# Scan of an RWKV-7 layer: 32x32 inverses from two 16x16 substitutions and two TensorE products, chunk products on 64 rows

## The chip, the cores and the metric

The kernel runs on one core of a Trainium2 chip. The metric is the time of one execution in microseconds (us) on the device. PE is the matrix engine, PEld its weight loads, DVE, ACT and POOL the vector, scalar and GpSimd engines, SP the engine whose queue issues most of the DMAs. Each engine takes its instructions in the order in which they stand for it, and waits on semaphores for the others.

## The reference

One inference step of a two-layer trunk: layer 0 mixes tokens with a bidirectional RWKV-7 scan, layer 1 with neighbourhood attention, each is followed by an MLP. There are 128 prompt tokens and 512 sample tokens, 16 heads of 64. What the change touches is the scan, run forward and backward:

```python
def delta_rule_scan(r, w, k, v, kk, a, s0, reverse):
    def step(S, inp):
        sa = jnp.einsum('bhvk,bhk->bhv', S, -kk_t)
        S_new = (S * w_t[:, :, None, :] + sa[..., None] * (kk_t * a_t)[:, :, None, :]
                 + v_t[..., None] * k_t[:, :, None, :]).astype(S.dtype)
        y = jnp.einsum('bhvk,bhk->bhv', S_new, r_t)
```

## The kernel before

All of it is float32; large products are made of exact pairs of reduced-precision factors. In the order of time: adaLN and the projections (to 320 us), the v product together with the preparation of the scan's first step (to 437), the scan (to about 823), the output projection (to 907), then MLP, attention and MLP.

**The scan in chunks.** Tokens go in five steps of 128 (n = 0 is the prompt, 1 to 4 the sample), each of four chunks of 32 tokens (e = 0 to 3), both directions d side by side, all 16 heads. Inside a chunk the rule above is a triangular system: with N the strictly triangular 32x32 products of a chunk, one per head, chunk and direction, TT is the transposed inverse of (I - N). `chain_step` (from L983) does a chunk of one direction: R on PE, its copy Rc on ACT, U = TT products (PE, 32 blocks on 32x32 positions, written A<-Rc,TT in the trace), GU copies on ACT, the state product (B<-GU,C) with its factor on DVE, and Y added on DVE (L1049).

**Preparation.** It runs one step ahead, in units of four head pairs, one direction and a window of 64 tokens, eight units a step. `prep_elem` (L882) makes decays (scan on DVE, L898) and the scaled KB and C tiles on POOL (L914, L929). Of a C tile, the rows that belong to the other head are filled with zeros, on ACT (L921) for one head and on POOL (L924) for the other, since `prep_group` (L943) multiplies over all 128 rows: 8 products (16 records; a float32 matmul shows as two) for each of two groups of a unit, on PE as pp<-C,KB. ACT copies N out of PSUM into invA, DVE masks the rest into C (L959). `fill` (L865) deals groups out between the stages of `chain_step`, four in a chunk.

**Inversion.** When a step's eighth unit is through, `invert` (L962) takes all its 128 blocks at once, one per partition: DVE masks N (L966), transposes (L967), and substitutes row by row (L975, L978: 30 rows, each a product into invT and an addition into invX, cut in two column halves from row 11 on, so 50 + 50 operations), then transposes into TT (L980). On DVE other operations stand between the rows where the emission order puts them. The inversion of step n+1 stands in step n, after its second chunk; the first step's stands in the v product.

**Order.** PE products of the scan go through `mm` (L832), which keeps them in the order in which they are written. On the other engines the order of emission stands. In the last step the post-processing of finished tokens (`post_half`, from L1096) and the first half of the output projection (`wo_first`, L1164) stand among the chunks; the latter's operands wx are loaded over SP's queue from what `post_half` has stored, and its residual input tiles wr rotate over three buffers.

## Time and profile before

| | |
|---|---|
| three runs | median 2279.94 us (2279.73 to 2282.37) |
| span of the profiled execution | 2277.6 us |
| busy share of the span | PE 89%, PEld 81%, DVE 53%, ACT 38%, POOL 24% |
| chain that ended last | PE 64%, DVE 11%, DMA 4%, POOL 3%, ACT 2% |
| DVE in that chain | L978 and L975 2% each, L959 1% |
| of POOL in it | L929 2% |

Busy times of one engine do not add to others; a share of the whole span hides which engine ends the waiting in a given stretch. So the scan is read in stretches that begin and end with a step's first or third chunk. In a timeline, the bracket at a row's end is the engine's idle time ahead of it and what ended it. PEclk is the granted clock of PE in tenths or as a share of its full 2.4 GHz.

### The profile page before, as it was taken

To read this page: it belongs to the slowest core of one execution; us is meant where nothing else is said; L and a number is where in the kernel's file an instruction comes from. 1 tells how busy PE (TensorE), PEld (TensorE's weight loads), DVE (VectorE), ACT (ScalarE), POOL (GpSimd) and SP (SyncE) were. 2 spreads that over 40 slices of the span, in tenths; PEclk is the share of its full clock that TensorE was granted. 3 is DMA by queue.
4 is the path that set the end of the run, shared out by engine and by line. 5 is a ranking of instruction groups with operands and counts; after the bars stand their busy time and mean duration, and the time that the engine had idled before them with its cause. 6 is when DMAs were issued, how large, how long until landed. Compare 5 with 4: busy or idle time off the path is not lost.

```text
span 2277.6 us, 44909 instructions
## 1 busy us (share of the span) xinstructions
PE 2022.0 (89%) x18516; PEld 1836.7 (81%) x18516; DVE 1198.3 (53%) x2593; ACT 866.0 (38%) x1734; POOL 544.3 (24%) x602
## 2 busy tenths in 40 slices
PE   5898978875567567999999999999999999999999
PEld 2687867754456457899999999888777999999999
DVE  6838574676886865433333335334566643434342
ACT  3435454355454334322232233222476431313130
POOL 2404368465552143101010010000132110101010
PEclk8597979988788788899999999999899999999999
DMA  6344855454443454322222323443411232222221
GB/s 229 103 131 131 252 186 163 127 165 141 139 138 117 106 165 136 122 93 93 93 86 91 93 75 94 142 129 94 138 43 32 78 120 75 75 75 75 75 75 73
DMA packets 161388, 260.01 MB, mean 114 GB/s; under 512 B 46880, under 2 KB 103328, under 8 KB 161184
## 3 DMA queue, kind: packets, MB, share of 16 engines
q1 hardware_dynamic: 146816, 240.37, 33.9%
q10 hardware_dynamic: 14368, 16.78, 2.2%
q8 instruction: 145, 2.38, 0.4%
q14 instruction: 59, 0.48, 0.1%
HBM read 218.18 MB, written 37.35 MB: 112 GB/s over the span
## 4 chain that ended last, share of the span: by engine, by line
PE 64%; DVE 11%; DMA 4%; POOL 3%; ACT 2%; issue 2%; SPq 1%; ACTq 0%; DVEq 0%; POOLq 0%
PE psl L205 48%; PE psl L239 3%; DVE invX L978 2%; PE ps L1497 2%; DVE invT L975 2%; POOL C L929 2%; PE po L1534 2%; PE pp L834 2%; PE pt L1522 2%; DVE C L959 1%; PE pp L1201 1%; PE psl L286 1%; PE A L834 1%; DMA ld_s<-scr 1%; PE psl L1238 1%
## 5 line engine op out<-in xcount | busy, mean ns | idle before, releaser
L191 ACT CAST whi<-wraw 128x1024 fp32r<-128x1024 f32 x179 | 187.2, 1048 | 727.6 <-PE psl L205 696.3
L205 PE MATMUL psl<-xh,whi 128*128 128x320 f32 (+1 forms) x1712 | 422.4, 320 | 20.1 <-ACT whi L191 14.5
L205 PE MATMUL psl<-xl,whi 128*128 128x320 f32 (+1 forms) x1712 | 419.1, 318 | 10.3 <-POOL xl L248 5.4
L205 PE MATMUL psl<-xh,wlo 128*128 128x320 f32 (+1 forms) x1712 | 415.7, 316 | 2.2 <-DVE wlo L193 2.2
L205 PEld LDWEIGHTS psl<-xh,whi 128*128 128x128 f32 x1712 | 297.2, 193 | 40.8 <-ACT whi L191 18.8
L205 PEld LDWEIGHTS psl<-xl,whi 128*128 128x128 f32 x1712 | 297.4, 193 | 18.2 <-POOL xl L248 7.5
L205 PEld LDWEIGHTS psl<-xh,wlo 128*128 128x128 f32 x1712 | 298.6, 193 | 4.6 <-DVE wlo L193 2.6
L1317 POOL TENSOR_TENSOR relu<-relu 128x640 f32<-128x640 f32 x64 | 80.6, 1261 | 753.5 <-ACT relu L1316 748.8
L1154 DVE SCALAR_TENSOR_TENSOR xres<-psl,mods,xres 128x320 f32<-128x320 f32 (+2 forms) x216 | 81.7, 434 | 305.5 <-PE psl L205 305.5
L205 PE MATMUL psl<-hhh,wlo 128*128 128x320 f32 x1024 | 233.4, 309 | 0.0
L205 PE MATMUL psl<-hhl,whi 128*128 128x320 f32 x1024 | 233.3, 309 | 0.0
L205 PE MATMUL psl<-hhh,whi 128*128 128x320 f32 x1024 | 233.2, 309 | 0.0
L193 DVE TENSOR_TENSOR wlo<-wraw,whi 128x1024 fp32r<-128x1024 f32 x179 | 222.6, 1246 | 9.6 <-ACT whi L191 9.2
L205 PEld LDWEIGHTS psl<-hhh,whi 128*128 128x128 f32 x1024 | 171.2, 188 | 0.4 <-issue 0.4
L205 PEld LDWEIGHTS psl<-hhh,wlo 128*128 128x128 f32 x1024 | 171.2, 188 | 0.0
L205 PEld LDWEIGHTS psl<-hhl,whi 128*128 128x128 f32 x1024 | 171.1, 188 | 0.0
L834 PE MATMUL pp<-C,KB 128*64 128x128 f32 x1280 | 103.3, 313 | 41.3 <-DVE C L959 17.6
L1274 DVE TENSOR_TENSOR relu<-psl,rms_b 128x320 f32<-128x320 f32 x128 | 60.8, 486 | 144.7 <-PE psl L205 143.6
L834 PEld LDWEIGHTS pp<-C,KB 128*64 128x64 f32 x1280 | 85.8, 158 | 54.2 <-issue 26.7
L248 DVE TENSOR_TENSOR hhl<-relu,hhh 128x640 fp32r<-128x640 f32 x64 | 53.4, 834 | 127.3 <-ACT hhh L247 127.2
L248 POOL TENSOR_TENSOR xl<-mixt,xh 128x640 fp32r<-128x640 f32 x36 | 67.3, 1873 | 135.6 <-ACT xh L247 126.6
L959 DVE TENSOR_TENSOR C<-pp,cstsb 64x512 f32<-64x512 f32 x80 | 55.0, 688 | 83.0 <-ACT C L956 69.2
(291 smaller groups left out, 3480.7 us busy)
## 6 DMA issues: line engine op xcount, KB each, us to landing
wraw<-in_mlp_w SPq DMA_DIRECT2D x128, 512.0 KB, 3.5
adaraw<-in_ada_w SPq DMA_DIRECT2D x96, 512.0 KB, 4.9
ld_d<-scr SPq DMA_DIRECT2D x20, 512.0 KB, 4.3
ld_s<-scr SPq DMA_DIRECT2D x20, 512.0 KB, 3.8
bias<-in_bias SPq DMA_DIRECT2D x16, 384.0 KB, 3.6
scr<-ta SPq DMA_DIRECT2D x16, 325.0 KB, 3.4
wi<-scr SPq DMA_DIRECT2D x20, 260.0 KB, 4.5
scr<-bp SPq DMA_DIRECT2D x16, 320.0 KB, 4.2
```

The source lines that it names most:

```text
L191: nc.scalar.copy(hi, raw)
L193: nc.vector.tensor_tensor(lo, raw, hi.bitcast(F32), op=ALU.subtract)
L205: self.nc.tensor.matmul(ps[g][:, :e - c], lhsT=a[:, k, :], rhs=b[:, c:e], start=(k == 0 and j == 0), stop=(k == n - 1 and j == 2))
L239: nc.tensor.matmul(ps, lhsT=a[:, tc_], rhs=w, start=(k == 0 and j == 0), stop=(k == KT - 1 and j == 2))
L248: (lo_eng or nc.vector).tensor_tensor(xl, src, xh.bitcast(F32), op=ALU.subtract)
L834: r = (op or self.nc.tensor.matmul)(*a, **k)
L929: nc.gpsimd.tensor_tensor(rev(o) if s == 0 else o, v4(sh, s, ww)[hs], f[hs], op=ALU.mult)
L959: nc.vector.tensor_tensor(C[o, 8 * h:8 * h + 8, :], pn[o, :, 0:64], mask[o], op=ALU.mult)
L975: nc.vector.tensor_tensor(t, X[:, s + 1:, s:s + 1].broadcast_to([P, m, b - a]), X[:, s:s + 1, a:b].broadcast_to([P, m, b - a]), op=ALU.mult)
L1154: nc.vector.scalar_tensor_tensor(out[:, a:b], ps[g][:, o:o + b - a], gate[:, k, j:j + 1], x[:, a:b], op0=ALU.mult, op1=ALU.add)
L1274: nc.vector.tensor_tensor(t[:, c], ps[q][:, :HALF], rb[:, c], op=ALU.mult)
L1317: nc.gpsimd.tensor_tensor(t, t, t, op=ALU.mult)
```

## The change

The diff below is cut to its core; elsewhere it only takes comments out.

The inverse of a block (I - N) is taken in parts. DVE substitutes the two 16x16 blocks on the diagonal together (14 rows, 28 operations). The block between them is the product of the second inverse, the coupling and the first: two sets of 128 products on PE (`invert_rest`), with ACT copying the first set's result into invS and DVE adding the second to half of TT. `invert_rest` is a generator: the first set is emitted at the third group of products after the inversion, the second at the next one, or both ahead of the first U that uses them (`invert_on`). DVE writes one transpose more, POOL clears three halves.

Chunk products take the 64 rows of one head, at positions that lie diagonally; the zero fill is gone. One stacked 64-wide identity replaces two half identities in the C tiles (25 slots, 26 before). `wo_first` rotates wr over two buffers.

```diff
@@ c_slots
-            c = pool.tile([P, 26, 64], F32, name=f"C{i}")
-            self.nc.any.tensor_copy(c[:, 16:18, :].rearrange("p a x -> p (a x)"), self.cst("ident"))
+            c = pool.tile([P, 25, 64], F32, name=f"C{i}")
+            self.nc.vector.tensor_tensor(c[:, 16], ident[:, :64], ident[:, 64:], op=ALU.add)
@@ fill
+            self.invert_on()
             u = self.units[self.m_i]
             self.prep_group(*u, self.m_g)
@@ prep_elem
-        for h in range(2):
-            z = C[64 - 64 * h:P - 64 * h, 8 * h:8 * h + 8, :]
-            if h:
-                nc.scalar.activation(z.rearrange("p a b -> p (a b)"), self.cst("scan1")[64 - 64 * h:P - 64 * h, :512],
-                                     AF.Copy, scale=0.0)
-            else:
-                nc.gpsimd.memset(z, 0.0)
@@ prep_group
-                self.mm(pv[r:r + 64, e, q, :], lhsT=KB[:, q, e].rearrange("p s t -> p (s t)"), rhs=C[:, n:17 + h:16 + h - n, :],
-                        start=True, stop=True, tile_position=(0, r))
+                hs = slice(64 * h, 64 * h + 64)
+                self.mm(pv[r:r + 64, e, q, :], lhsT=KB[hs, q, e].rearrange("p s t -> p (s t)"), rhs=C[hs, n:17:16 - n, :],
+                        start=True, stop=True, tile_position=(64 * h, r))
...
-            ts["D"] = self.inv.tile([P, 2, 8, 2, 32], F32, name="invA")
+            ts["D"] = self.inv.tile([P, 2, 8, 2, 32], F32, name="invA", bufs=2)
@@ invert
-        for s in range(1, 31):
-            m = 31 - s
-            cs = ((0, min(s, 10)), (10, s))[:1 + (s > 10)]
...
-            for t, (a, b) in zip(tv, cs):
-                nc.vector.tensor_tensor(X[:, s + 1:, a:b], X[:, s + 1:, a:b], t, op=ALU.add)
+        nc.gpsimd.memset(Xm[:, 16:32, 0:16], 0.0)
+        nc.gpsimd.memset(Dt[:, :, 0:16], 0.0)
+        Xd = X.rearrange("p (b r) -> p b r", b=2)[:, :, :512].rearrange("p b (t s) -> p b t s", s=32)[:, :, :, :16]
+        ST = self.inv.tile([P, 32, 32], F32, name="invS")
+        tmp = ST.rearrange("p a b -> p (a b)")
+        for s in range(1, 15):
+            m = 15 - s
+            t = tmp[:, :2 * m * s].rearrange("p (b m s) -> p b m s", b=2, m=m)
+            nc.vector.tensor_tensor(t, Xd[:, :, s + 1:, s:s + 1].broadcast_to([P, 2, m, s]),
+                                    Xd[:, :, s:s + 1, 0:s].broadcast_to([P, 2, m, s]), op=ALU.mult)
+            nc.vector.tensor_tensor(Xd[:, :, s + 1:, 0:s], Xd[:, :, s + 1:, 0:s], t, op=ALU.add)
+        nc.vector.transpose(ST.rearrange("p n s -> p s n"), Xm.rearrange("p t s -> p s t"))
+        nc.gpsimd.memset(ST[:, :, 16:32], 0.0)
         TT = self.ttp.tile([P, 32, 32], F32, name="TT")
-        nc.vector.transpose(TT.rearrange("p n t -> p t n"), X)
+        nc.vector.transpose(TT.rearrange("p n t -> p t n"), Xm)
         ts["TT"] = TT
+        self.inv_todo = ts, self.invert_rest(Dt, ST, TT)
+        self.inv_wait = 3
+
+    def invert_rest(self, D, ST, TT):
+        nc = self.nc
+        pz = self.pp_tile()
+        z = pz[:, :512].rearrange("p (n j) -> p n j", j=16)
+        w = pz[:, 512:].rearrange("p (n j) -> p n j", j=16)
+        for n in range(32):
+            for q in range(4):
+                self.mm(z[32 * q:32 * q + 32, n], lhsT=D[32 * q:32 * q + 16, n, :], rhs=ST[32 * q:32 * q + 16, n, 0:16],
+                        start=True, stop=True, tile_position=(32 * q, 32 * q))
+        nc.scalar.copy(ST[:, :, 0:16], z)
+        yield
+        for n in range(32):
+            for q in range(4):
+                qs = slice(32 * q, 32 * q + 32)
+                self.mm(w[qs, n], lhsT=ST[qs, n, :], rhs=TT[qs, n, 16:32], start=True, stop=True,
+                        tile_position=(32 * q, 32 * q))
+        nc.vector.tensor_tensor(TT[:, :, 16:32], TT[:, :, 16:32], w, op=ALU.add)
+
+    def invert_on(self, ts=None):
+        if ts is None:
+            self.inv_wait -= 1
+            if self.inv_todo and self.inv_wait <= 0 and next(self.inv_todo[1], 1):
+                self.inv_todo = None
+        while ts is not None and self.inv_todo and self.inv_todo[0] is ts:
+            if next(self.inv_todo[1], 1):
+                self.inv_todo = None
@@ chain_step
         yield
+        self.invert_on(ts)
         TT = ts["TT"]
@@ wo_first
-            xi = self.wf[min(k % 3, 1)].tile([P, NA], F32, name=f"wr{k % 3}")
+            xi = self.wf[k % 2].tile([P, NA], F32, name=f"wr{k % 2}")
```

Three places show how it moves instructions. First PE in the third chunk of step 0, from the second direction's U on (A<-Rc,TT is U, B the state product, pp<-C,KB a group of chunk products, x the count of matmuls). Before:

```order
L834 MATMUL A_4826<-Rc,TT 32x64 x16
L834 MATMUL A_4826<-cstsb,adasb 128x2 x2
L834 MATMUL pp_4850<-C_2767,KB 64x128 x16
L834 MATMUL B_3991<-GU_2749,C_2765 64x64 x4
L834 MATMUL B_3991<-GU_2749,C_2773 64x64 x4
L834 MATMUL A_4894<-GU_4005,C_2761 32x64 x8
L834 MATMUL A_4894<-GU_4005,C_2769 32x64 x8
L834 MATMUL A_4913<-GU_2749,C_2765 32x64 x8
```

After, in the same place (pp<-invS,invA is the first set, pp<-TT,invS the second):

```order
L836 MATMUL A_4907<-Rc,TT 32x64 x16
L836 MATMUL A_4907<-cstsb,adasb 128x2 x2
L836 MATMUL pp_4931<-invS,invA 32x16 x128
L836 MATMUL pp_5061<-C_2767,KB 64x128 x8
L836 MATMUL pp_4931<-TT,invS 32x16 x128
L836 MATMUL pp_5061<-C_2767,KB 64x128 x8
L836 MATMUL B_4157<-GU_2749,C_2765 64x64 x4
L836 MATMUL B_4157<-GU_2749,C_2773 64x64 x4
L836 MATMUL A_5234<-GU_4171,C_2761 32x64 x8
L836 MATMUL A_5234<-GU_4171,C_2769 32x64 x8
```

The first set now stands ahead of the group of chunk products, the second in the middle of it, and B behind both.

Second, DVE in the same chunk, the end of the substitution and what follows it, after (L976 and L978 are the substitution, L956 the mask of C, L979 the transpose into invS, L982 the one into TT, L1003 the addition to TT):

```order
L978 TENSOR_TENSOR invX<-invX,invS 128x2x3x12
L976 TENSOR_TENSOR invS<-invX 128x52
L978 TENSOR_TENSOR invX<-invX,invS 128x2x2x13
L956 TENSOR_TENSOR C_2759<-pp_4806,cstsb 64x512 x2
L976 TENSOR_TENSOR invS<-invX 128x28
L978 TENSOR_TENSOR invX<-invX,invS 128x2x14
L979 STREAM_TRANSPOSE invS<-invX 128x32x32
L982 STREAM_TRANSPOSE TT<-invX 128x32x32
L1082 TENSOR_TENSOR Y<-Y,A_4889 128x256
L300 TENSOR_TENSOR mods_90<-A_4907,parsb 128x4
L1003 TENSOR_TENSOR TT<-TT,pp_4931 128x32x16
L956 TENSOR_TENSOR C_2767<-pp_5061,cstsb 64x512 x2
```

The second transpose and the addition stand close behind the substitution, which has few other rows between its own; before, the 100 operations were spread over this chunk and the next, among the rows of both.

Third, DVE at the end of step 3, where the last inversion ends. Before (L980 is the transpose into TT, L1088 and L1093 the factors of the state, L1142, L1118 and L1124 to L1133 post-processing):

```order
L1142 TENSOR_TENSOR pbuf<-pp_8657,pbuf 128x256 x2
L978 TENSOR_TENSOR invX<-invX,invT_7954 128x10
L980 STREAM_TRANSPOSE TT<-invX 128x32x32
L1088 TENSOR_TENSOR GU_4008<-B_3991,FC 64x512 x2
L1093 TENSOR_TENSOR B_3991<-B_3991,FC 128x512
L1049 TENSOR_TENSOR Y<-Y,A_8532 128x256
L1124 TENSOR_REDUCE yvar<-pbuf 128x8
L1118 TENSOR_REDUCE ysum<-Y 128x8
L1125 TENSOR_SCALAR yvar<-yvar 128x8
L1174 TENSOR_TENSOR ww_9414<-adaraw,ww_9413 128x1024
```

After (L1162 to L1166 are the end of post-processing, L1003 the addition to TT, L1121 and L1126 the factors):

```order
L264 SCALAR_TENSOR_TENSOR yrs<-rsq_t_9594,rsq_i_9593 128x8
L1162 TENSOR_TENSOR Y<-Y,yrs 128x512
L1165 TENSOR_TENSOR Y<-Y,lnwb 128x512
L1166 TENSOR_TENSOR Y<-Y,pbuf 128x512
L1003 TENSOR_TENSOR TT<-TT,pp_9169 128x32x16
L1082 TENSOR_TENSOR Y<-Y,A_9488 128x256
L1082 TENSOR_TENSOR Y<-Y,A_9650 128x256
L1121 TENSOR_TENSOR GU_4171<-B_4156,FC 64x512 x2
L1126 TENSOR_TENSOR B_4156<-B_4156,FC 128x512
```

Post-processing that stood behind the last inversion stands ahead of its end. On PE both sets stand straight before step 4's first U there.

## Rows read from the trace of the kernel before

**Rows 1.** stretches: length; PE, PEld, DVE, ACT, POOL busy (count); PEclk, DMA share, GB/s
```profile
320.00:437.00 117.00, 97.57 (x900) 89.42 (x899) 75.43 (x168) 53.18 (x127) 75.76 (x104) 0.88 0.51 155
479.00:534.00 55.00, 26.50 (x700) 22.60 (x704) 53.59 (x141) 25.12 (x62) 31.37 (x46) 0.78 0.45 141
563.00:616.00 53.00, 27.43 (x684) 21.93 (x676) 51.80 (x142) 23.66 (x62) 34.88 (x47) 0.80 0.51 154
616.00:645.00 29.00, 25.87 (x685) 21.07 (x688) 11.04 (x16) 20.91 (x56) 13.26 (x21) 0.89 0.43 137
645.00:689.00 44.00, 27.35 (x680) 22.91 (x680) 42.16 (x122) 21.12 (x57) 23.46 (x29) 0.81 0.35 114
718.00:761.00 43.00, 23.13 (x560) 18.47 (x560) 42.42 (x150) 13.71 (x31) 11.24 (x9) 0.70 0.32 90
```
**Rows 2.** timeline of PE, third chunk of step 0: start, duration, records [idle <- releaser]
```profile
482.38 1.09 PE L834 MATMUL pp<-C,KB 128*64 128x128 f32 x16
...
485.90 0.65 PE L834 MATMUL A<-Rc,TT 32*32 32x64 f32 x32 [0.18 <-ACT Rc L1017]
...
489.56 3.46 PE L834 MATMUL pp<-C,KB 128*64 128x128 f32 x32 [2.48 <-DVE C L959]
492.95 1.15 PE L834 MATMUL B<-GU,C 64*64 64x64 f32 x32
...
497.09 0.65 PE L834 MATMUL A<-Rc,TT 32*32 32x64 f32 x32 [1.96 <-ACT Rc L1017]
```
**Rows 3.** timeline of PE: first products after its longest waits, steps 1 to 3
```profile
533.52 1.07 PE L834 MATMUL A<-Rc,TT 32*32 32x64 f32 x32 [18.83 <-DVE rsq_t L262]
...
616.12 1.08 PE L834 MATMUL A<-Rc,TT 32*32 32x64 f32 x32 [13.66 <-DVE TT L980]
...
682.77 3.68 PE L834 MATMUL pp<-C,KB 128*64 128x128 f32 x32 [10.35 <-DVE invX L978]
```
**Rows 4.** groups by line: forms, count | busy, mean ns | idle before: the substitution, DVE
```profile
L978 DVE TENSOR_TENSOR invX<-invX,invT 128x38 f32<-128x38 f32 (+14 forms) x250 | 80.7, 351 | 1.2
...
L975 DVE TENSOR_TENSOR invT<-invX 128x108 f32<-128x108 f32 (+14 forms) x250 | 74.1, 325 | 1.3
```
**Rows 5.** timeline of DVE in the same chunk, where step 1's inversion begins
```profile
478.67 1.23 DVE L966 TENSOR_TENSOR invA<-invA,cstsb 128x1024 f32<-128x1024 f32 x1
...
481.84 1.96 DVE L967 STREAM_TRANSPOSE invX<-invA 128x1024 f32<-128x1024 f32 x1
483.88 0.17 DVE L975 TENSOR_TENSOR invT<-invX 128x30 f32<-128x30 f32 x1
...
484.79 0.72 DVE L975 TENSOR_TENSOR invT<-invX 128x58 f32<-128x58 f32 x1
...
490.50 0.32 DVE L975 TENSOR_TENSOR invT<-invX 128x150 f32<-128x150 f32 x1
...
491.45 1.23 DVE L898 TENSOR_TENSOR_SCAN wi<-cstsb,wi 128x520 f32<-128x520 f32 x1
...
495.77 1.39 DVE L959 TENSOR_TENSOR C<-pp,cstsb 64x512 f32<-64x512 f32 x2
```
**Rows 6.** groups by line: the zero fill on ACT and POOL
```profile
L921 ACT ACTIVATE C<-cstsb 64x512 f32<-64x512 f32 x40 | 23.8, 624 | 1.5 <-PE A L834 1.1
...
L924 POOL MEMSET C<- 64x512 f32 x40 | 20.6, 527 | 5.1 <-PE A L834 4.7
```
**Rows 7.** waits of PE from 320 to 437: total us, times, longest
```profile
PE pp L834 <- POOL C L929: 8.7, 5, 3.3
```
**Rows 8.** timeline of PE, then DVE and SP's queue, in the last step
```profile
761.34 1.07 PE L834 MATMUL A<-Rc,TT 32*32 32x64 f32 x32 [1.36 <-DVE TT L980]
...
801.92 0.69 PE L1201 MATMUL pp<-wx,ww 128*128 128x384 f32 x1 [5.43 <-ACT wx L1186]
...
779.17 0.69 DVE L1133 TENSOR_TENSOR Y<-Y,pbuf 128x512 f32<-128x512 f32 x1
...
799.05 1.58 SPq L1183 DMA_DIRECT2D adaraw<-scr  x3
```

More of the change, by code (lines that the diff above doesn't have):

```diff
@@ L710, in c_slots @@
     def c_slots(self, pool, n, par):
+        ident = self.cst("ident")
         for i in range(n):
[L713 to L714 removed]
+            c = pool.tile([P, 25, 64], F32, name=f"C{i}")
+            self.nc.vector.tensor_tensor(c[:, 16], ident[:, :64], ident[:, 64:], op=ALU.add)
             self.free[par].append(c)
@@ L742, in scan_pools @@
         self.pin = False
+        self.inv_todo, self.inv_wait = None, 0
     def pp_tile(self, i=None):
@@ L955, in prep_group @@
                                pv[64 - 64 * h:96 - 64 * h, :, b:4:2, 0:32])
-        nc.scalar.copy(C[:, 18:26, :], pn[:, :, 64:P])
+        nc.scalar.copy(C[:, 17:25, :], pn[:, :, 64:P])
         for h in range(2):
@@ L963, in invert @@
         nc = self.nc
-        X = self.inv.tile([P, 32, 32], F32, name="invX")
+        X = self.inv.tile([P, 1056], F32, name="invX")
+        Xm = X[:, :1024].rearrange("p (t s) -> p t s", s=32)
         Dt = ts["D"].rearrange("p d g l t -> p (d g l) t")
         nc.vector.tensor_tensor(Dt, Dt, self.cst("dmask").unsqueeze(1).broadcast_to([P, 32, 32]), op=ALU.mult)
-        nc.vector.transpose(X, Dt.rearrange("p n t -> p t n"))
-        nc.vector.memset(X.rearrange("p a b -> p (a b)")[:, 0:1024:33], 1.0)
@@ L969, in invert @@
-        tmp = [self.inv.tile([P, 256], F32, name=f"invT{i}") for i in range(2)]
-        for s in range(1, 31):
-            m = 31 - s
-            cs = ((0, min(s, 10)), (10, s))[:1 + (s > 10)]
-            tv = [t[:, :m * (b - a)].rearrange("p (a b) -> p a b", b=b - a) for t, (a, b) in zip(tmp, cs)]
-            for t, (a, b) in zip(tv, cs):
-                nc.vector.tensor_tensor(t, X[:, s + 1:, s:s + 1].broadcast_to([P, m, b - a]),
-                                        X[:, s:s + 1, a:b].broadcast_to([P, m, b - a]), op=ALU.mult)
-            for t, (a, b) in zip(tv, cs):
-                nc.vector.tensor_tensor(X[:, s + 1:, a:b], X[:, s + 1:, a:b], t, op=ALU.add)
+        nc.vector.transpose(Xm, Dt.rearrange("p n t -> p t n"))
@@ new lines, in invert @@
+        nc.vector.memset(X[:, 0:1024:33], 1.0)
+        nc.gpsimd.memset(Xm[:, 16:32, 0:16], 0.0)
[9 more added lines that the diff above has]
+            nc.vector.tensor_tensor(Xd[:, :, s + 1:, 0:s], Xd[:, :, s + 1:, 0:s], t, op=ALU.add)
@@ L1073, in state_update @@
                 for hp in range(2):
-                    i = 18 + 4 * ee + 2 * (ph % 2) + pp
+                    i = 17 + 4 * ee + 2 * (ph % 2) + pp
                     self.mm(G[hs(hp), pp, ph, :], lhsT=C[ph // 2][ho(hp), i, :], rhs=gu[ho(hp), hp, pp, ph, :],
```

## The prediction

> **What bounds the kernel now.** I read the span in stretches first, and from there the waits of the stretch that the change touches. Behind the output projection, for six tenths of the span, PE is busy nearly all the time and no line of the diff runs there; that stays. The scan (437 to 823) alternates between two limits [rows 1]. Of the four chunks of a step, the first two are paced by PE: 25.9 of 29 us busy, DVE 11. The last two are paced by DVE: 53.6 of 55 us in step 0, 51.8 of 53 in step 1, 42.2 of 44 in step 2, 42.4 of 43 in step 3, with PE busy 23 to 27. The reason is the inversion of the next step's 32x32 blocks: 500 small operations, 74.1 + 80.7 = 154.8 us [rows 4], 31 us for each of five inversions. It begins when the third chunk begins (478.67 in [rows 5]). PE then waits 18.8 us and 13.7 us before the first product of the next step, and 10.4 us in step 2 for a group's products, and comes back at half the pace (1.07 us for 32 records instead of 0.65; 3.68 for 32 chunk products, [rows 2, 3]). So a cheaper inversion can pay at most where DVE is the limit, and it must not push its work onto PE at the wrong place.
>
> **The change part by part.**
>
> *DVE work removed.* 100 operations an inversion become 28, all dependent, of 28 to 112 elements. In the third chunk of step 0, 14 substitution operations stand between 483.88 and 491.45 [rows 5]; less 1.4 us for the mask of C and 0.3 for two small ones, that is 5.9/14 = 0.42 us each, contended ones (0.72 us at 58 elements) and quiet ones (0.32 at 150) mixed. I take 0.40, since the new ones are shorter: 28 x 0.40 = 11.2 us. The bounds are 28 x 0.32 = 9.0 and 28 x 0.72 = 20.2. A second transpose (1.96, the row of L967) and one addition of 128x512 (0.7, half of the 1.39 of a mask pair) come on top. DVE is relieved of 31 - 11.2 - 2.7 = 17 us a step. This is no saving of time yet.
>
> *The two products on PE.* Each is 128 small matmuls, 256 records, on 32x32 positions. The nearest row is U: 32 records on 32x32 positions in 0.65 us [rows 2]. So 8 x 0.65 = 5.2 us each at the high clock and 8 x 1.07 = 8.6 at the low one [rows 3]; with fewer columns (16 for 64) it could be less, 2.6 by a halving that no row shows. I take 6.2 for the first, which starts after an idle stretch, and 5.2 for the second.
>
> *Where they stand.* In steps 0 to 2 the first product stands in PE's order in the third chunk, behind the second direction's U and ahead of the chunk products that before started at 489.56 [rows 2]. Its operand is the second transpose, at the end of the substitution. PE works in order, so everything behind it waits: the group's products, B, A, and the whole fourth chunk. From the mask of N at 478.67: 5.2 us to the substitution (483.88), 11.2 for it, 1.2 for a scan, 1.4 for a mask pair and 0.7 for B's factor that stand between its rows, 2.0 for the transpose: 21.7. Then 6.2 (first product), 1.2 (ACT's copy beside half a group, 1.09 by [rows 2]), 5.2 (second product), 1.1 (the other half), 1.15 (B), 1.1 (A), 2.0 (the wait for Rc before 497.09): 39.6, or 39.3 from the chunk's start. The fourth chunk then has no DVE work worth waiting for and takes half of a PE-paced pair, 29/2 = 14.5. The pair: 53.8 us. Step 0 had 55, step 1 53, step 2 44. In step 2 I take 52.5, since its POOL is less busy (23.5 of 44 against 31.4 of 55, [rows 1]). Against this, the next step starts warm: 1.07 - 0.65 for U and about 0.9 for the 16 products behind it, so -1.3 in steps 0 and 1, and -1.8 in step 2 (3.68 for 32 falls to 2 x 1.09, less 0.3 for what the clock still loses). Step 0: -1.2 - 1.3 = **-2.5**. Step 1: 0.8 - 1.3 = **-0.5**. Step 2: 8.5 - 1.8, about **+6.5**. So the 17 us of DVE that are freed in each are given back, since the substitution was spread over two chunks beside PE's work and is now waited for in one.
>
> *Step 3 and the last step.* Here both products stand after all chunk work, straight before the first U of step 4 (761.34, [rows 8]), and the addition to TT stands on DVE behind the post-processing of the finished tokens, which before ran after that U, up to 779.17 + 0.69. DVE was busy 42.4 of 43 us from 718 to 761 [rows 1] and went on without a pause. From 718 to 779.86 are 61.9 us; less 31, plus 11.2 and 2.7, less some 2 us of step 4's own operations: 42.8. The addition ends near 761, so U starts where it did, **0** (-4 to +5). But the post-processing is now done by then, and the chunks of step 4 lose DVE's delays: about 3 us in the first chunk. The outputs go out about 5 us earlier, and with them the queue on SP that loads them back (799.05); PE's wait of 5.43 us at 801.92 for wx [rows 8] falls away for the most part. I take **-6.5** for both, with -12 to 0 as bounds (0 if the loads stay behind what precedes them on SP).
>
> *Zero fill.* 40 fills of 0.62 us on ACT and 40 of 0.53 on POOL go [rows 6]. ACT has room everywhere. POOL is near its limit only while the first step is prepared: 75.8 of 117 us with PE waiting 8.7 us for its C tiles [rows 7]. Eight fills of 0.53 are 4.2 us of that. In the same stretch the first inversion's products add 10.4 us to PE, which is busy 97.6 of 117; the idle 19.4 takes some of it. I put 4.2 against 4.2: **0** (-6 to +10). In steps 0 and 1 POOL's fills end no long wait of PE; **-2** (-4 to 0). Three small fills an inversion come back on POOL, the last of which waits for the second transpose with what is queued behind it.
>
> *Chunk products on 64 rows.* The same number of records. Before, 32 records of 128 columns in two column halves took 2 x 1.09 us, 68 ns each. B already uses 64x64 positions that lie diagonally, into one accumulator, at 36 ns for 64 columns [rows 2], about the same per column. **0** (-1 to +2 a step).
>
> The Trainium skill, "TensorEngine Tiling (Array Packing)", section "Gotcha 1: PSUM Pressure", says that row tiles may not write one PSUM bank at the same time, so that such pairs would run one after the other. B's row speaks against it: 36 ns at 64 columns is no slower per column than the full-height products. By that rule each of 1,280 records would take up to twice 68 ns.
>
> *The residual's input tiles.* Three become two. A load then waits for the store two tiles back instead of three. The load is wanted only by the addition behind a tile's products. **0** (0 to +8, the size of the wait for wx and half as much again).
>
> **Sum.** -2.5 - 0.5 + 6.5 - 6.5 + 0 - 2 + 0 = -5.0 us. The profiled execution has a span of 2277.6 us, 2.3 below the median of 2279.94, so I apply it to the median: **2275 us**.
>
> **The rivals.**
>
> *DVE relief goes through.* If the substitution ends at 9 us and hardly anything delays it, or the first product is quicker than U's row says, the pair falls towards the work of PE alone: 26.5 + 11.4 = 38 us plus some 5 of short waits, 43 us. Step 0 -12, step 1 -10, step 2 -2, step 3 -6, with the other terms (-8.5) about -35: 2240 to 2256. For it: PE and DVE are each busy under 40 us then. Against it: PE's order, with 14 us from the second U to the transpose and nothing in between.
>
> *Slower: PE stands at the first product.* Each microsecond by which the transpose comes later is paid in steps 0 to 2 in full, so the change turns slower than before from 1.7 us later on (5.0/3), and by over 0.2% from 3.2 us. At 0.60 us an operation (+5.6 us), and the first product at the low clock (+2.4), it is 3 x 8 = +24: 2299; half of that gives 2287. For it: operations of 0.72 us next to POOL's, and POOL is busy 31.4 of 55 us there. Against it: 0.42 is measured in the same place.
> The Trainium skill, "SBUF — State Buffer", section "Who interferes with whom", says that a two-input DVE operation and a GpSimd operation that reads SBUF block each other for a whole instruction. The rows of 0.72 beside 0.32 fit. It would put all 28 operations near 0.72 only if POOL never paused.
>
> *Row pairs run one after the other.* If the 64-row products lose their overlap, 1,280 records at up to 68 ns more are +87 us on PE, of which at least half falls where PE paces: 2320 to 2360. B's row speaks against it.
>
> *The tail gives it back.* Two input tiles stop the output projection in each of the last tiles: +5 to +8, so 2280 to 2283.
>
> **How the numbers follow.** My sum, 2275 with 2264 to 2286 by the smaller bounds: 0.56, of which 0.29 below 2275.4, 0.25 within 0.2% (4.6 us, about what a measurement of this kernel can tell from no change), 0.02 above. DVE relief goes through: 0.16, all faster. PE stands at the product: 0.20, of which 0.17 slower by over 0.2%. Serial row pairs: 0.03. The tail: 0.05, all within 0.2%. Together: faster 0.45, within 0.33 (with 0.03 of the slower rival's mild end), slower 0.22. The range leaves out the far ends of both rivals: 2252 to 2296 holds 0.56 + 0.07 + 0.05 + 0.14, about 0.8.
>
> **What the profile after would show.** If I am right: DVE in the last two chunks of steps 0 to 2 is at 35 to 40 us instead of 42 to 54; PE has one wait of 10 to 15 us before the 32x16 products, released by the transpose; the wait before a step's first U is gone; each pair takes 52 to 55 us. The 28 operations last 10 to 13 us. The wait for wx is below 3 us. Wrong: pairs of 43 us (relief), a wait of over 18 us before the product (slower), 16 chunk products above 1.5 us at the high clock (serial pairs), or products of 32x16 far from 5 us for 256 records.

## The result, and the profile after

The changed kernel takes **2364.14 us** (median of 2346.39, 2351.58, 2376.70, 2378.62) against 2280.12 before: ratio 1.0368, 95% interval 1.0307 to 1.0429. The forecast was 2275, with 2252 to 2296 as its range: wrong in sign and far outside. The profiled execution (2376.70, span 2374.9) is 97.3 us longer than that of before (2277.6).

One milestone splits the 97.3: the first product of attention. PE's timelines, before and after, start and duration in front:

```profile
1613.55 0.70 PE L1497 MATMUL ps<-kT,qT 64*128 64x256 f32 x4
```
```profile
1681.12 0.70 PE L1530 MATMUL ps<-kT,qT 64*128 64x256 f32 x4
```

67.6 us are lost ahead of it, 29.7 behind it. The 29.7 lie in code that the diff doesn't touch (last section). The 67.6 arise in the scan. Its four chunks a step, each measured from one first U of direction 0 to the next, in us:

| | step 0 | step 1 | step 2 | step 3 | sum |
|---|---|---|---|---|---|
| before | 18.9, 22.3, 18.2, 36.4 | 15.6, 13.8, 24.3, 29.0 | 15.0, 13.8, 18.4, 25.7 | 12.3, 16.9, 20.2, 23.0 | 323.7 |
| after | 36.1, 13.5, 40.2, 16.2 | 28.0, 13.5, 43.2, 19.9 | 24.2, 13.9, 38.6, 14.5 | 12.3, 19.5, 25.1, 35.1 | 393.8 |

That is +70.2: the first chunks +38.8, the second -6.4, the third and fourth together +37.6 (1.8, 9.8, 9.0 and 17.0 by step). The rest of the scan takes 6.4 less (from step 4's first U to the last U, 50.6 instead of 56.9), the way from there to attention 2.7 more, and the first U comes 1.1 later.

The stretches after (length; PE, PEld, DVE, ACT, POOL busy; granted clock, DMA share, GB/s): step 0's first chunk, then the third and fourth chunk of steps 0, 1, 2 and 3, to set beside [rows 1].

```profile
438.77:474.87 36.10, 18.89 (x351) 12.72 (x352) 6.02 (x8) 11.28 (x29) 17.76 (x27) 0.72 0.51 154
488.40:544.81 56.41, 36.27 (x1192) 31.09 (x1193) 30.09 (x58) 20.99 (x54) 19.63 (x32) 0.73 0.34 105
586.31:649.40 63.09, 37.53 (x1196) 32.09 (x1196) 32.53 (x71) 21.60 (x57) 27.66 (x38) 0.72 0.40 111
687.50:740.57 53.07, 36.01 (x1192) 31.46 (x1192) 27.56 (x55) 19.85 (x54) 18.77 (x30) 0.71 0.30 97
772.37:832.60 60.23, 28.69 (x1072) 24.27 (x1073) 48.40 (x121) 14.70 (x32) 11.77 (x12) 0.65 0.34 92
```

DVE's relief is there: 28 to 33 us busy in a pair of steps 0 to 2, where it had 53.6 and 51.8 in the first two. In these pairs, and in the first row, no engine is near its limit: in the first row PE is busy 18.9 of 36.1 us, DVE 6, ACT 11, POOL 18. (In step 3 DVE is still busy 48 of 60 us.) So the waits have to be read. Those of PE in the scan (437 to 870; total, times, longest), first after, then before:

```profile
PE A L836 <- ACT Rc L1049: 45.6, 16, 10.8
PE B L836 <- ACT GU L1067: 27.5, 7, 13.3
```
```profile
PE A L834 <- ACT Rc L1017: 13.7, 15, 2.2
```

Waits for these two short copies of ACT in the chain of states, 16 us before (2.6 of them for GU), are 73 us now. The longest shows why. DVE, ACT and PE after, in step 0's first chunk:

```profile
465.05 1.24 DVE L901 TENSOR_TENSOR_SCAN wi<-cstsb,wi 128x520 f32<-128x520 f32 x1 [12.87 <-DMA wi<-scr]
466.21 0.14 DVE L300 TENSOR_TENSOR mods<-A,parsb 128x4 f32<-128x4 f32 x1
```
```profile
466.32 0.64 ACT L902 ACTIVATE w<-wi 128x520 f32<-128x520 f32 x1 [12.69 <-DVE wi L901]
467.05 0.64 ACT L903 ACTIVATE wi<-wi 128x520 f32<-128x520 f32 x1
467.71 1.55 ACT L1067 ACTIVATE GU<-A 32x256 f32<-32x256 f32 x4
```
```profile
468.91 2.37 PE L836 MATMUL B<-GU,cstsb 128*64 128x512 f32 x4 [13.30 <-ACT GU L1067]
```

The running sum of a coming window (`prep_elem`) waits 12.9 us on DVE for a load, its exponential 12.7 us on ACT for the sum, and the GU copy that PE needs stands behind both. In before's trace the same operations stand the other way round: GU and the small addition to `mods` first, the sum and the exponentials 13 us later, beside the chain. The sum itself starts at about the same time in both (464.19 and 465.05); what changed is what stands behind it:

```profile
450.98 0.16 DVE L300 TENSOR_TENSOR mods<-A,parsb 128x4 f32<-128x4 f32 x1 [1.23 <-PE A L834]
...
464.19 1.24 DVE L898 TENSOR_TENSOR_SCAN wi<-cstsb,wi 128x520 f32<-128x520 f32 x1 [8.16 <-DMA wi<-scr]
```
```profile
451.17 1.55 ACT L1034 ACTIVATE GU<-A 32x256 f32<-32x256 f32 x4 [0.33 <-DVE mods L300]
...
465.46 0.64 ACT L899 ACTIVATE w<-wi 128x520 f32<-128x520 f32 x1 [8.92 <-DVE wi L898]
```

The diff doesn't touch these lines. Here a sentence ahead of the prediction is wrong: on the engines other than PE it is not the order of emission that stands. The kernel's TileContext is opened with `schedule_with_timeline_sim=True`: by this flag's name the scheduler plays the program on a timeline of its own and sets the order of ACT, DVE, POOL and SP's queue by it; only PE is tied by `mm`. That this timeline came out another way with the edits is inferred from the changed order, in which preparation moved ahead of the chain; no run switches the flag off.

### The profile page after: what moved, and what is told of

The parts are those of the page before. It is cut to its first block, busy times and chain, and to the rows that moved or that the text cites. A ratio compares the mean times of both kernels' runs of the same rounds, so it can differ in the third digit from the quotient of the medians.

```text
span 2374.9 us, 49634 instructions
## 1 busy us (share of the span) xinstructions
PE 2097.0 (88%) x21076; PEld 1895.8 (80%) x21076; DVE 1134.0 (48%) x2250; ACT 849.7 (36%) x1692; POOL 520.6 (22%) x577
## 3 DMA queue, kind: packets, MB, share of 16 engines
q1 hardware_dynamic: 146816, 240.37, 31.7%
## 4 chain that ended last, share of the span: by engine, by line
PE 64%; DVE 5%; DMA 5%; POOL 3%; issue 3%; ACT 2%; SPq 1%; ACTq 0%; DVEq 0%; POOLq 0%
PE psl L205 45%; PE psl L239 3%; PE pp L836 3%; PE ps L1530 3%; PE po L1567 2%; POOL C L925 2%; PE pt L1555 2%; DMA wi<-scr 1%; PE A L836 1%; PE psl L286 1%; PE pp L1234 1%; PE B L836 1%; DMA adaraw<-in_ada_w 1%; DMA scr<-pbuf 1%; DVE C L956 0%
## 5 line engine op out<-in xcount | busy, mean ns | idle before, releaser
L205 PEld LDWEIGHTS psl<-xh,whi 128*128 128x128 f32 x1712 | 296.3, 193 | 37.1 <-ACT whi L191 14.8
L248 DVE TENSOR_TENSOR hhl<-relu,hhh 128x640 fp32r<-128x640 f32 x64 | 53.4, 834 | 127.4 <-ACT hhh L247 127.3
L836 PE MATMUL pp<-C,KB 64*64 64x128 f32 x1280 | 101.8, 306 | 10.4 <-POOL C L925 6.1
L956 DVE TENSOR_TENSOR C<-pp,cstsb 64x512 f32<-64x512 f32 x80 | 55.1, 689 | 113.5 <-ACT C L953 97.7
L836 PEld LDWEIGHTS pp<-C,KB 64*64 64x64 f32 x1280 | 83.6, 152 | 23.0 <-issue 12.6
```

The lines of the kernel that those rows point to most:

```text
L205: self.nc.tensor.matmul(ps[g][:, :e - c], lhsT=a[:, k, :], rhs=b[:, c:e], start=(k == 0 and j == 0), stop=(k == n - 1 and j == 2))
L248: (lo_eng or nc.vector).tensor_tensor(xl, src, xh.bitcast(F32), op=ALU.subtract)
L836: r = (op or self.nc.tensor.matmul)(*a, **k)
L956: nc.vector.tensor_tensor(C[o, 8 * h:8 * h + 8, :], pn[o, :, 0:64], mask[o], op=ALU.mult)
```

## The experiments

Theory one (**order**): the chain waits because operations that wait for a load were put ahead of it on engines that work in order. Theory two (**resource**): the preparation itself is late or dearer (loads, C tiles, KB products, PE's half-height products). A separate question is what the two sets of products cost. Beside the medians, the sum of steps 0 to 3 is given (first U of step 0 to first U of step 4; 323.7 before, 393.8 after), or the way from first to last U (380.6 and 444.4). Each is read from one profiled execution.

**e1, the chunk part alone.** The kernel before with the 64-row products, 25 slots and no zero fill; its inversion as it was.

```diff
-  rhs=C[:, n:17 + h:16 + h - n, :], tile_position=(0, r)
+  rhs=C[hs, n:17:16 - n, :], tile_position=(64 * h, r)
-  zero fill (activation, memset)
```

> The chunk products over 64 rows without zero fill, with the old inversion and three residual tiles. Before, the stretch from the first U of step 0 to the first U of step 4 takes 323.7 us (437.69 to 761.34), with the whole change 393.8 us (438.77 to 832.60). If the new inversion is the cause of the loss (its products stand in PE's order ahead of chunk work), this kernel is at 2275 to 2285 us and that stretch at 320 to 326. If the rival holds, that the dropped fills and the new places of the decays' operations on ACT and SP's queue cost the time, it takes 2320 us or more. If row pairs on 64 rows ran one after another, a group of 32 records would take well over 2 us at the high clock.

2318.93 us, 1.0184 (1.0160 to 1.0209); steps 0 to 3 364.5. More than half of the loss in these steps (+40.9 of 70.2) comes with a part that the prediction put at nothing, with no set of products in the kernel. (By the start of attention it is half, 33.7 of 67.6: e1's first U comes 8.0 earlier than before's.) Its trace has the same stop as the changed kernel's, DVE in step 0's first chunk:

```profile
456.37 1.24 DVE L899 TENSOR_TENSOR_SCAN wi<-cstsb,wi 128x520 f32<-128x520 f32 x1 [12.90 <-DMA wi<-scr]
457.52 0.14 DVE L300 TENSOR_TENSOR mods<-A,parsb 128x4 f32<-128x4 f32 x1
```

**e8 and e2, the fills put back**, in e1 and in the whole changed kernel.

> The chunk part of the change without dropping the zero fill: products over 64 rows, 25 slots, the fills still made although nothing reads them; old inversion. Against e1_chunks (2319 us, 364.5 us from the first U of step 0 to that of step 4) it differs by the fills alone, against the kernel before (2279, 323.7) by the products' rows. If dropping the fills makes the 40 us, because the operations on ACT, POOL and SP's queue then stand at other places, this kernel returns to within 10 us of the kernel before. If it stays above 2310, it is the products or the identity's slots, and the fills are not the cause.

> The whole change, with the zero fills made as before. If the fills' absence shifts the order on ACT and SP's queue and this costs the long first chunks (36.1, 28.0 and 24.2 us in steps 0 to 2, before 18.9, 15.6, 15.0), these return to 20 us or less and the total falls by 30 to 40 us. If not, the first chunks stay within 4 us of 36, 28 and 24.

e8: 2323.63, 1.0202 (1.0181 to 1.0223), 366.0. e2: 2351.09, 1.0331 (1.0287 to 1.0375), 397.5. It isn't the fills: with them back, the 64-row products on tiles of 25 slots (with the identity made on DVE) alone bring the loss.

**e3, both sets late**: only ahead of the first U that uses them.

```diff
-        self.inv_wait = 3
+        self.inv_wait = 99
```

> The whole change, with both sets of products emitted only ahead of the first U that uses them, in every step as it already is in step 3. If PE's wait at the first set in the third chunk makes the loss, the stretch from the first U of step 0 to that of step 4 falls from 393.8 to 350 us or less, by some 10 us a step, though 10 to 12 us for both sets then stand ahead of each first U. If the loss comes from loads and decays that arrive late, the stretch stays within 10 us of 393.8, and the waits of PE are ended by ACT copies as before.

2353.27, 1.0324 (1.0305 to 1.0343); 443.5 from first to last U against 444.4. PE's standing is only moved: the third chunks of steps 0 to 2 take 31.7 us less together than after, the first 29.8 less, and the fourth, at whose end both sets now stand, 60.1 more.

**e5 and e6, no load of the decay exponents**, after and before: the running sum runs over a constant, so its values are others.

```diff
-            nc.sync.dma_start(wi, self.tz_d[d][tt, :, hg])
-            nc.vector.tensor_tensor_scan(wi, self.cst("scan1"), wi, ...)
+            nc.vector.tensor_tensor_scan(wi, self.cst("scan1"), self.cst("scan1"), ...)
```

> The whole change, without the load of the decay exponents (wi): the running sum on DVE reads a constant instead, so the decays are not those of the inputs; all other operations stay. If the loss comes from the chain wi load, running sum, exponentials on ACT, with the chain's copies queued behind the exponentials, the stretch from the first U of step 0 to that of step 4 falls from 393.8 to 350 us or less. If PE's wait at the first set of products makes it, the stretch stays above 380.

> The kernel before, without the load of the decay exponents, in the same way (a constant is summed). With the inversion spread over two chunks as the limit there, the loads are hidden: the stretch of 323.7 us falls by less than 15 us by either theory. If it falls by much more, the loads cost as much in the kernel before, and cannot explain the difference.

One run each: e5 2327.48 with 380.7, e6 2291.01 with 323.1. In e5 the sum waits for the next late thing in its place, the tiles that POOL's C products free, and the addition stands behind it still (DVE of e5):

```profile
463.21 1.24 DVE L900 TENSOR_TENSOR_SCAN wi<-cstsb 128x520 f32<-128x520 f32 x1 [8.04 <-POOL C L924]
464.37 0.14 DVE L300 TENSOR_TENSOR mods<-A,parsb 128x4 f32<-128x4 f32 x1
```

So that load is not the cause by itself.

**e11, e10 and e12, the place of the KB products on POOL**: held ahead of C in e1 (e11) and after (e10), behind C in before (e12). SP's next load waits for them.

```diff
+  tc.add_manual_dep(<first of C / of KB>, <last of KB / of C>, order only)
```

> The chunk part alone (as e1_chunks), with the KB products kept on POOL ahead of the C tiles of the same window, as they mostly stand in the kernel before. In e1_chunks and e8_k64 two of eight KB products a double unit have moved behind four C products; SP's queue then waits 99 to 107 us in the scan for KB to free the tile of ld_d (24 us in the kernel before), with the loads of wi and of the chain's values queued behind. If that is the cause of the 40 us, this kernel is at 2275 to 2295 us and that wait under 50 us; if not, it stays above 2310.

> The whole change with KB kept ahead of the C tiles on POOL. If the place of KB costs the long first chunks, their 36.1, 28.0 and 24.2 us fall to 25 or less and the five steps from 393.8 us to 350 to 370; what stays over 323.7 is then PE's wait at the two sets of products. If it stays above 385, the place of KB is not it.

> The kernel before, with the KB products of a pair of units put behind the C products of its first unit on POOL; nothing else changed. If a late KB holds the tile of ld_d and with it SP's queue, this makes the kernel before slower by 20 to 50 us, with SP's wait for KB at 80 us or more and long first chunks. If the place of KB is harmless, it stays within 10 us of 2279.

e11 2312.26, 1.0156 (1.0131 to 1.0181), 359.0; e10 2338.61, 1.0275 (1.0249 to 1.0301), 394.5; e12 2282.00, 1.0020 (1.0005 to 1.0035), 336.9. A small share: held, it takes 5.6 of e1's 40.9 us back and none of the whole change's 70.2 (e10's shorter time lies outside these steps, most of it in attention and behind). Put into before it costs 13.2 in steps 0 to 3, of which 3.3 are left when attention starts.

**e9, e14, e16 and e17, the exponentials held on ACT behind a GU copy.** e14 (in e1), e16 (after) and e17 (e3) hold them behind the last GU copy written before them; e9 (after) also writes a window's preparation at the end of the chunk.

```diff
+  tc.add_manual_dep(<exponential>, <last GU copy>, order only)
```

> The whole change, with the decays of coming units emitted at a chunk's end and their two exponentials kept, on ACT, behind the GU copies of the second direction. In the whole change they stand ahead of these copies in step 0 (466.32, released by the running sum, then GU at 467.71), and the second direction's U waits. If that place is the loss, the first chunk of step 0 falls from 36.1 to 20 to 25 us and the five steps lose 20 us or more of 393.8. If loads and buffers pace the preparation whatever the place, the sum of a step's four chunks stays within 4 us of 106, 105, 91 and 92.

> The chunk part alone (as e1_chunks), with only this added: the two exponentials of a coming unit may not stand on ACT ahead of the GU copies that were written before them. From the first U to the last, the kernel before takes 380.6 us, e1_chunks 422.4, and ACT stands idle at the head of its queue for an exponential (waiting for the running sum) for 23.6 and 69.8 us. If that place makes the loss, this kernel takes 385 to 400 us there and is at 2280 to 2297 us, with that idle time under 40 us. If the preparation is late whatever the order on ACT, it stays above 2308 and the idle time moves to another engine's queue.

> The whole change, with the same order for the exponentials. From the first U to the last the whole change takes 444.4 us, 22 more than e1_chunks. If the place of the exponentials makes the 40 us, this falls to 400 to 425 and what remains over the kernel before is the two sets of products; if not, it stays within 8 us of 444.

> The whole change with both sets of products only ahead of the next step's first U (as e3_late, 443.5 us from the first U to the last) and the exponentials' order kept. If the two losses are separate, this takes 400 us or less and could come near the kernel before; if the late sets give back what the order gains, it is within 8 us of e16_exps_after.

e9 2349.08, 1.0348 (1.0286 to 1.0410), 440.3 from first to last U; e14 2321.35, 1.0196 (1.0169 to 1.0223), 365.5; e16 2361.45, 1.0353 (1.0309 to 1.0398), 406.6; e17 2350.54, 1.0328 (1.0300 to 1.0356), 439.1 from first to last U. None brings the time back, and the theory in this form, the place of the exponentials alone, falls. But e14's trace says why. DVE, then ACT:

```profile
459.60 1.24 DVE L900 TENSOR_TENSOR_SCAN wi<-cstsb,wi 128x520 f32<-128x520 f32 x1 [13.10 <-DMA wi<-scr]
460.76 0.14 DVE L300 TENSOR_TENSOR mods<-A,parsb 128x4 f32<-128x4 f32 x1
```
```profile
460.93 1.54 ACT L1032 ACTIVATE GU<-A 32x256 f32<-32x256 f32 x4 [12.66 <-DVE mods L300]
```

The exponential is out of the way, and GU waits 12.66 us all the same: for the addition to `mods` on DVE, which stands behind the waiting sum. The order is wrong on two engines at once, and DVE's alone is enough to stop the chain.

**e18, e19 and e21, both held.** The preparation is written behind the second direction's U; the sum is held behind the last `mods` addition on DVE, the exponentials behind the last GU copy on ACT. e18 is e1 with this, e19 the whole changed kernel, e21 the kernel before.

```diff
+  tc.add_manual_dep(<running sum>, <last mods addition>, order only)
+  tc.add_manual_dep(<exponential>, <last GU copy>, order only)
-  while self.e_i < len(self.units) and ...:   # prep_elem
+  while (last or not self.dve_chain) and self.e_i < len(self.units) and ...:
```

> The kernel before with the chunk part alone (as e1, 2318.9 us), and the preparation of a window (running sum on DVE, the two exponentials on ACT) written behind the second direction's U and held behind the last `mods` addition on DVE and the last GU copy on ACT. If the chunk part costs 40 us because a running sum that waits for its load stands ahead of a chain operation on DVE or ACT, the five steps come from 364.5 us back to 325 to 340, the idle time ahead of the `mods` addition and of GU goes, and the time is 2280 to 2295. If the preparation is late whatever its order (its loads and the tiles of POOL set it), the waits move to the products of the chunk and the time stays at 2312 to 2325.

> The changed kernel with the same writing and the same two holds. Head-of-line waits: 2364 or 2350 less 25 to 40, 2310 to 2335, with the waits at the first product and in the third and fourth chunks left. Preparation late whatever its order: 2340 to 2365.

> The kernel before with the writing and the two holds of e18. If what is left in e18 (2299.5, or 24 us over before) is the price of the holds themselves, this is at 2290 to 2300 and the chunk part costs nothing once the order is the same; if it is a cost of the chunk part, this is at 2272 to 2283.

| | order as scheduled | | | both held | | |
|---|---|---|---|---|---|---|
| | time | steps 0 to 3 | attention starts | time | steps 0 to 3 | attention starts |
| before | 2280.12 | 323.7 | 1613.55 | 2283.50 (e21) | 330.5 | 1613.40 |
| chunk part | 2318.93 (e1) | 364.5 | 1647.23 | 2299.46 (e18) | 348.5 | 1632.43 |
| whole change | 2364.14 | 393.8 | 1681.12 | 2311.76 (e19) | 369.5 | 1649.88 |

Ratios of the held ones: e21 1.0029 (1.0015 to 1.0043), e18 1.0101 (1.0067 to 1.0134), e19 1.0155 (1.0127 to 1.0183). With the late writing and two order-only holds, and no work changed, attention starts 31.2 us earlier in the whole change, 14.8 in the chunk part, and where it did in before. The medians fall by 52 and 19 us and rise by 3 (6 against before's own runs beside e21, 2277.39); by difference some 20 of the 52 lie behind attention's start, where the clock differed (last section). So order at these places is shown to be a cause. How much it makes is seen against before with the same holds: in steps 0 to 3 the chunk part's loss falls from 40.9 to 18.0, the whole change's from 70.2 to 39.0, about half of either. That it is the larger part of the whole loss is not shown. Nor is it shown which of the three does it; e9, which has ACT's hold and a late writing but not DVE's hold, had gained little.

e19 lies in the range that this theory gave. e18 came in short of its 2280 to 2295, so order at these two places isn't all; by e21 about a quarter of what is left there is the price of the holds (6.9 of 24.8 us in steps 0 to 3). What became of PE's waits in e19 (437 to 870):

```profile
PE A L839 <- ACT Rc L1057: 17.6, 15, 2.4
...
PE B L839 <- ACT GU L1075: 7.1, 5, 3.2
```

73 us have become 25. In their place stands a wait that before and after don't have, for KB from POOL, which preparation now brings late; e19, then e21, which has it too:

```profile
PE pp L839 <- POOL KB L926: 26.4, 6, 5.2
```
```profile
PE pp L837 <- POOL KB L923: 28.8, 6, 5.3
```

So what theory two names is there in all three held kernels, in before as well, and doesn't tell them apart. In e18 step 0's first chunk is as in before: the addition at 444.16, GU at 444.35 after 0.33 us of idle; the sum runs at 458.75, in the second chunk, straight behind that chunk's addition.

What is left in the chunk part, 18.0 us in steps 0 to 3 (348.5 against 330.5), was followed in one place, step 1's third chunk (35.2 against 28.7). There ACT of e18 waits until a store of post-processing has left the tile that it is to write (scr<-pbuf), with GU's and Rc's copies queued behind it; in e21 the same operation ran at 552.71 without a wait.

```profile
563.02 0.63 ACT L1126 ACTIVATE pbuf<-Y 128x512 f32<-128x512 f32 x1 [9.63 <-DMA scr<-pbuf]
```

It is the same kind of stop by another operation. That all 18 us are of this kind is argued, not shown; no run held the post-processing. The other 21.0 us of e19 come with the new inversion, 15.0 of them in step 3's last two chunks (60.8 us, 45.8 in e18).

**e22, step 3's sets inside its fourth chunk.** e19 with the first set ahead of the second direction's first products and the second behind them.

```diff
+                    if (n, e) == (3, 3):
+                        self.inv_wait = 0
+                        self.invert_on()
                     next(s1)
+                    if (n, e) == (3, 3):
+                        self.invert_on()
```

> e19 (2311.8), with the two sets of 128 products of step 3 written inside the fourth chunk, ahead of the second direction's first products and behind them, and no longer ahead of step 4's first U. In e19 the way from the first set to that U is 21 us (786.16 to 807.30), of which 10.3 are waits for ACT's copy and DVE's addition. If that way is paid in full, the time falls by 10 to 18 us, to 2294 to 2302; if the fourth chunk is late for another reason, by less than 5.

2325.23, 1.0213 (1.0190 to 1.0237): slower than e19, against both expectations. Steps 0 to 3 fall from 369.5 to 359.6 us, the fourth chunk of step 3 from 35.8 to 31.1. But the first three chunks of step 4 rise from 40.5 (7.9, 10.2, 22.4) to 50.1 (16.9, 12.6, 20.6), and from first to last U only 1.4 us are gained. When the sets are early, post-processing is late in step 4: in its first chunk PE waits 5.97 us for an activation of post-processing on ACT that itself waits 4.64, with GU's copies behind it. So the way through the sets is not what sets the end alone. The longer time arises behind the scan, 5.9 us from the last U to attention and 6.6 from there on; its cause was not followed.

## Why the prediction was wrong, point by point

**What held.** *The sets' own price, in size.* PE after, step 0's third chunk, beside [rows 2]:

```profile
506.84 1.08 PE L836 MATMUL A<-Rc,TT 32*32 32x64 f32 x32 [10.77 <-ACT Rc L1049]
...
510.56 2.32 PE L836 MATMUL pp<-invS,invA 16*32 16x16 f32 x158 [1.69 <-DVE invS L979]
514.27 1.56 PE L836 MATMUL pp<-invS,invA 16*32 16x16 f32 x98 [1.39 <-issue]
515.76 1.97 PE L836 MATMUL pp<-C,KB 64*64 64x128 f32 x16
517.67 2.10 PE L836 MATMUL pp<-TT,invS 32*32 32x16 f32 x141
521.09 1.78 PE L836 MATMUL pp<-TT,invS 32*32 32x16 f32 x115 [1.32 <-issue]
```

The first set lasts 510.56 to 515.83, 5.3 us, the second 5.2 (517.67 to 522.87); 6.2 and 5.2 were put down. The working under it is another: it took 0.65 us for 32 records, U's price at 2.4 GHz, and the sets of steps 0 to 2 ran at 1.2, for which it had 8.6. The stretch of the first set (columns as in [rows 1]):

```profile
510.56:515.83 5.27, 3.88 (x258) 3.74 (x259) 1.95 (x3) 1.50 (x4) 0.44 (x1) 0.50 0.02 6
```

PE is busy 3.88 us of it, 15 ns a record against U's 33 at that clock (1.07/32), and a gap of 1.4 us comes on top. Narrower records, the lower clock and the gap happen to make 5.2. *The substitution.* All five inversions, by line:

```profile
L978 DVE TENSOR_TENSOR invX<-invX,invS 128x28 f32<-128x28 f32 (+6 forms) x70 | 23.1, 330 | 1.9
L976 DVE TENSOR_TENSOR invS<-invX 128x28 f32<-128x28 f32 (+6 forms) x70 | 22.9, 327 | 1.9
```

46.0/5 = 9.2 us an inversion, against 11.2 taken and 9.0 as the lower bound. From the mask of N (487.50) to the end of the transpose into invS (510.41) are 22.9 us against the working's 21.7, a wait for the sum's load among them. *Products on 64 rows.* 1,280 records, before and after:

```profile
L834 PE MATMUL pp<-C,KB 128*64 128x128 f32 x1280 | 103.3, 313 | 41.3 <-DVE C L959 17.6 <-POOL C L929 11.8 <-DVE invX L978 10.3
```
```profile
L836 PE MATMUL pp<-C,KB 64*64 64x128 f32 x1280 | 101.8, 306 | 10.4 <-POOL C L925 6.1 <-issue 3.3 <-DVE C L956 1.0
```

No loss, as B's row in [rows 2] had said: row pairs one after the other are not to be seen. The Trainium skill, "TensorEngine Tiling (Array Packing)", "Gotcha 1: PSUM Pressure", says that row tiles can't access one PSUM bank at the same time; by that rule they would have run so, and this trace doesn't agree.

**What held by luck.** *The pairs of steps 0 to 2, once the order is mended:* 53.4, 55.1 and 50.4 us in e19, against 53.8, 53.8 and 52.5 forecast. That DVE's relief brings no time stands there (e21's pairs, with the old inversion, take 47.0, 52.7 and 45.7). That it is given back in PE's wait at the first set does not: the waits there are 3.3, 6.4 and 3.6 us, and 5.2 us in each pair are the wait for KB. *The third chunk.* The third chunk of step 0 takes 40.2 us, forecast 39.3. But PE was to wait 10 to 15 us at the first set; it waits 1.69 there, and 10.77 ahead of U for Rc, which on ACT stands behind an exponential that waits 11.40. A right length with another wait in it is no proof of the reason.

**The step that failed: "chunk products 0".** This term priced the products themselves, and as such it was right. What it left out is that such an edit lets the scheduler set another order for everything around it. (The zero fill's term did not fail: with the fills back, e8 and e2, the loss stays. Ahead of the scan, where 4.2 us gained stood against 4.2 lost, e1's first U comes 8.0 us earlier and the whole change's 1.1 later than before's.) Of the places that the prediction compared, two were on DVE at the inversion and one on PE; ACT, and DVE and SP's queue at the preparation, were not looked at, since their order was taken to be that of the code. The cost: 40.9 us in steps 0 to 3 with the chunk part alone (e1), of which the holds take 16.0 back, and 24.3 of the 70.2 of the whole change (e18, e19). What the rest of the chunk part's loss is stays open, beyond the one place shown above. It was also why the first chunks (+38.8) had no term at all. That the first two chunks are "paced by PE" had been read in step 2 (25.9 of 29 us); in step 0 PE was busy 31.0 of 41.2 before. Which detail of the products or of the tiles turns the scheduler's order was not taken apart.

**The second step that failed: step 3, "U starts where it did, 0 (-4 to +5)".** It measured +17.0, and with the order held still +17.6 (60.8 against 43.2 for the pair, or 41.1 in e21). The working had the addition to TT end with DVE's post-processing near the old time and put both sets in PE's idle time, with no price for the hops between them. In fact the first set stands in PE's order behind all of the fourth chunk, and all that follows is one chain: set, ACT's copy, set, DVE's addition, U. PE after, then ACT and DVE:

```profile
811.85 1.56 PE L836 MATMUL pp<-invS,invA 16*32 16x16 f32 x164
815.51 1.46 PE L836 MATMUL pp<-invS,invA 16*32 16x16 f32 x92 [2.10 <-issue]
824.24 2.42 PE L836 MATMUL pp<-TT,invS 32*32 32x16 f32 x164 [7.27 <-ACT invS L996]
827.97 1.46 PE L836 MATMUL pp<-TT,invS 32*32 32x16 f32 x92 [1.30 <-issue]
832.60 1.07 PE L836 MATMUL A<-Rc,TT 32*32 32x64 f32 x32 [3.17 <-DVE TT L1003]
```
```profile
823.09 0.63 ACT L1155 ACTIVATE pbuf<-Y 128x512 f32<-128x512 f32 x1 [10.26 <-DMA bc<-scr]
823.62 0.57 ACT L996 COPY invS<-pp 128x512 f32<-128x512 f32 x1
```
```profile
831.26 0.69 DVE L1166 TENSOR_TENSOR Y<-Y,pbuf 128x512 f32<-128x512 f32 x1
831.87 0.68 DVE L1003 TENSOR_TENSOR TT<-TT,pp 128x512 f32<-128x512 f32 x1
```

20.75 us from set to U (811.85 to 832.60). ACT's copy of 0.57 us stands behind an activation that waits 10.26 us, by the profile for post-processing's load, and the addition behind three operations of post-processing. The order listing ahead of the prediction showed the addition standing there; it was read as harmless. e22 shows a limit of this account: with the sets early, the fourth chunk falls by 4.7 us only.

**The tail.** Put at -6.5 together with step 3. Step 4's part measured -6.4 (50.6 against 56.9), for the reason given: post-processing is done by then. But the wait for wx didn't shrink; it went from 5.43 [rows 8] to 7.1 us, and the way to attention is 2.7 longer. Two input tiles cost at most that; in e19, which has two as well, that way is 3.2 shorter than before.

**The rivals.** "PE stands at the first product" (2287 to 2299) named the right kind of stop, an engine in order behind a late operand, on the wrong engine and with a third of the size (24 us of 70). The parts of "DVE relief goes through" add up to -38.5, not to about -35; nothing hangs on it. Serial row pairs (2320 to 2360) held the lower half of the runs by number, and for a mechanism that isn't there. The range was worked out from prices of single operations; nothing in it stood for a new order.

## What to carry to other kernels

Where a scheduler sets the order, compare the order of every engine that the critical chain touches, not only at the lines of the diff: look for an operation that waits for a load standing ahead of one that the chain needs. An edit of cheap work can bring that about, and holding one engine's order (ACT's here) doesn't help while a second one has the same fault. When work is split over engines, cost every hop of it where nothing else is left to run, and what is queued ahead of each hop.

## What the runs showed of the hardware that was not expected

PE's clock stayed at its lower level under full load. Attention after (columns as in [rows 1]; PEclk is the third number from the end), then before, then e6:

```profile
1681.00:1700.00 19.00, 12.93 (x66) 9.42 (x64) 13.33 (x42) 10.74 (x33) 5.06 (x9) 0.70 0.66 235
1700.00:1764.00 64.00, 64.00 (x247) 43.15 (x247) 25.21 (x94) 27.19 (x80) 11.23 (x21) 0.50 0.09 25
1764.00:1790.00 26.00, 26.00 (x173) 18.52 (x173) 16.84 (x64) 18.15 (x55) 7.20 (x13) 0.94 0.11 31
```
```profile
1623.00:1633.00 10.00, 9.95 (x46) 6.96 (x45) 6.14 (x31) 7.85 (x25) 4.74 (x9) 0.51 0.46 160
1633.00:1700.00 67.00, 67.00 (x459) 47.84 (x459) 45.89 (x179) 49.77 (x152) 20.83 (x38) 1.00 0.16 49
```
```profile
1630.00:1650.00 20.00, 20.00 (x82) 13.55 (x78) 7.60 (x24) 7.75 (x22) 2.62 (x5) 0.50 0.00 1
```

The granted clock is 0.50 (1.2 GHz) for 64 us in which PE is busy without a gap, where before it came back to 1.00 after 10 us at 0.51 of the same code: about 30 us, the 29.7 behind the milestone. The changed kernel's four runs lie in two pairs, 2346 to 2352 and 2377 to 2379, 27 us apart, which would fit; only one of them has a trace, so that is not shown. In the traces of the other versions of the changed kernel, which started attention at 1650 to 1694 us, it took 661 to 668 us from there to the end, as before (664.0). It isn't the change alone that can bring it: e6, the kernel before without one load, has it too, and takes 679.1 there. What sets it off stays open.

The sets of 128 small products came with gaps for which the profile names only "issue", 1.2 to 2.1 us once in every set of the changed kernel; U's row, from which they were priced, has none.
